# Independent products put ahead of transposes that wait, in a two-layer decoder trunk on one core

## The chip, the cores and the metric

The kernel runs on one core of a Trainium2 chip. The metric is device time in microseconds (us) of one launch, as the median of several runs; the trace comes from one profiled execution. The engines are called TensorE (PE in the profile; PEld is its weight load), VectorE (DVE), ScalarE (ACT), GpSimd (POOL) and SyncE (SP, here only a queue that issues loads).

## The reference

The input is 512 tokens of width 1024, and a memory of 256 rows. There are two layers, and everything is float32:

```python
for layer in range(2):
    x = layer_norm(a * x + 0.5 * swiglu(x, ffn_w_gu[layer, 0], ffn_w_down[layer, 0]))
    if layer == 0:   # latent attention: 12 heads from a low-rank q (256) and kv (128)
        o_tok, q_mem = mla_mix(x, ...)
    else:            # sparse attention: compressed, selected and window branches
        o_tok, q_mem = nsa_mix(x, ..., *shared)
    o_mem = memory_attention(q_mem, mem, w_mem_kv[layer])
    x = layer_norm(a * x + concat(o_tok, o_mem) @ w_out[layer])
    x = layer_norm(a * x + 0.5 * swiglu(x, ffn_w_gu[layer, 1], ffn_w_down[layer, 1]))
    if layer == 0:
        shared = nsa_shared_kv(x, nsa_w_kv, cmp_pos, cmp_w1, cmp_b1, cmp_w2)
```

In `mla_mix` one product `x @ w_in` gives the low-rank q and kv, a rotary key of 32 and the memory queries (256). The q and kv parts are normed (rms). In `nsa_shared_kv` one product gives keys and values; for the compressed branch, overlapping windows of 32 rows (stride 16) of the keys (j = 0) and of the values (j = 1) go through a small network:

```python
def compress(z, j):                       # 31 windows, two groups
    flat = (z[:, :, idx] + cmp_pos[j]).reshape(B, G, n_cmp, 32 * 64)
    return jax.nn.gelu(flat @ cmp_w1[j] + cmp_b1[j]) @ cmp_w2[j]
```

In `nsa_mix`, one product gives queries, 36 gates for each token and the memory queries.

## The kernel before, in words

A float32 product is made of three products: each operand is cast to a high half on ScalarE, VectorE subtracts it from the source to get the low half (`split`, lines 198 and 199), and TensorE adds high times high, high times low and low times high (`mm3`, lines 350 to 352, with the token tile standing still; `feature_major`, lines 362 to 367, with the weights standing still). The feed-forwards use a scheme with fewer products for part of their tiles (lines 375 to 379).

Weights arrive in units of 128 by 1024 numbers, in the fixed order of `_unit_order`. `unit(name, idx, look)` hands out the next unit and prepares up to `look` more: `prep` issues the load on SP's queue (line 129) into one of 4 raw buffers and splits it into one of 7 pairs of buffers. So a unit's load waits until a raw buffer is split, its split waits until a pair is free, and a pair is free when TensorE has made its last product with it.

The program is written in the order of the stages; a scheduler then sets the final order of each engine's instructions once, from the written order as priority and a model of its own. Each engine runs its list in order. PSUM banks are named by number, `bank(i)`. The stages are: feed-forward, memory keys, `mla_in`, latent heads, output product, feed-forward, `shared_kv`, feed-forward, `nsa_in`, sparse heads, output product, feed-forward. The change touches four places:

- **The latent step (`mla_in`).** For each of 4 token tiles t: 24 products into `bank(t)` with 416 columns; ScalarE sums squares; GpSimd takes the power; VectorE writes the scaled tile `c` (lines 762 to 771); TensorE transposes it in four pieces into `bank(4 + t)` (line 776); then `split`. Behind the loop come the two halves of the memory queries, 48 products each.
- **The compressed keys (`shared_kv`).** Behind the key products: 24 products of values for each of 4 token tiles (from the units `wvv`), then for j = 0 and 1: 48 products of the windows `zz[j]` with four units `w1`, the gelu on VectorE and ScalarE (lines 984 to 991, its result is `hb`), two transposes of `hb` (line 994), a split into `hT`, and 6 small products with the unit `w2`. Between the loads on SP's queue stand two copies of the keys (`ke`, `ko`, lines 963 and 964), each waiting for its cast.
- **Layer 1's first step (`nsa_in`).** For each token tile, 24 products of 292 columns; ScalarE takes the gates' exponential and copies the memory queries into `c` (line 1071), a buffer that it shares with the layer norms' gain and bias; TensorE transposes `c` (line 1074). Query products stand between the second and the third tile.
- **The start.** 12 products of zeros warm TensorE (line 1256), `prep()` loads the first weights, then eight pieces of the transposed input are loaded (line 1262) and split into `xhi` and `xlo`. The constants `cst` are loaded on GpSimd's queue, and VectorE casts them to `cbf` (line 1269).

Of the kernel before, what the change touches and what calls it, by code (L numbers as in the profile page):

```python
# [17 lines left out]
P = 128  # L18
T = 512
D = 1024  # L20
NT = 4
# [31 lines left out]
def _unit_order():  # L53

    order = []

    def ffn(l, f, s):
        for m0, items in _groups(l, f):
            m = m0
            for it in items:  # L60
                if it == "d":
                    order.extend((f"g{i}", (l, f, m), 1024, s) for i in range(4))
                else:
                    order.extend(("gu", (l, f, m, g), 1024, s) for g in range(2))
                m += 1
            for i in range(m0, m):
                order.append(("dn", (l, f, i), 1024, s))

    ffn(0, 0, 0)
    for l in range(2):  # L70
        for i in range(4):
            order.append(("wm", (l, i), 1024, 0))
    for i in range(4):
        order.append(("wc", (i,), 832, 0))
    for i in range(2):
        order.append(("wqm", (i,), 1024, 0))
    order.append(("wuv", (), 768, None))
    order.append(("wuk", (), 768, None))
    for i in range(3):
        order.append(("wuq", (i,), 1024, None))  # L80
    for k in MIXORDER:
        order.append(("wo", (0, k), 1024, 1))
    ffn(0, 1, 1)
    for i in range(4):
        order.append(("wkf", (i,), 1024, 1))
    for i in range(2):
        order.append(("wvv", (i,), 1024, 1))
    for j in range(2):
        for i in range(4):
            order.append(("w1", (j, i), 1024, 1))  # L90
        order.append(("w2", (j,), 256, 1))
    ffn(1, 0, 1)
    for i in range(3):
        order.append(("wgq", (i,), 876, 1))
    for i in range(6):
        order.append(("wq", (i,), 1024, 1))
    for k in MIXORDER:
        order.append(("wo", (1, k), 1024, 2))
    ffn(1, 1, 2)
    return order  # L100
# [3 lines left out]
def tile_trunk(ctx: ExitStack, tc, a: dict, out):  # L104
# [633 lines left out]
    def mla_in(cT):  # L738
        tst, tp = right_pool("mtmp", 2)
        rope = tp.tile([P, 2, NT, 32], F32, name="rope", bufs=1)  # L740
        nc.gpsimd.dma_start(rope, a["rope"])
        gbc = tp.tile([P, 384], F32, name="gbc", bufs=1)
        nc.gpsimd.dma_start(gbc[:, 0:256], a["mla_q_norm_g"].to_broadcast([P, 256]))
        nc.gpsimd.dma_start(gbc[:, 256:384], a["mla_kv_norm_g"].to_broadcast([P, 128]))
        ws = [unit("wc", (i,), 3 - i) for i in range(4)]
        for t in range(NT):
            ps = bank(t)
            q = slice(t * P, (t + 1) * P)
            for k in range(NKT):
                hi, lo = ws[k // 2]  # L750
                c = slice(k % 2 * 416, k % 2 * 416 + 416)
                mm3(ps[:, 0:416], F.xhi[:, k, q], F.xlo[:, k, q], hi[:, c], lo[:, c], k == 0, k == NKT - 1)
            ss = tp.tile([P, 2], F32, name="ss")
            junk = tp.tile([P, 256], F32, name="junk", bufs=1)
            nc.scalar.activation(junk, ps[:, 0:256], AF.Square, accum_out=ss[:, 0:1])
            nc.scalar.activation(junk[:, 0:128], ps[:, 256:384], AF.Square, accum_out=ss[:, 1:2])
            nc.vector.tensor_scalar(ss[:, 0:1], ss[:, 0:1], 1.0 / 256, RMS_EPS, op0=ALU.mult, op1=ALU.add)
            nc.vector.tensor_scalar(ss[:, 1:2], ss[:, 1:2], 1.0 / 128, RMS_EPS, op0=ALU.mult, op1=ALU.add)
            rr = tp.tile([P, 2], F32, name="rr")
            nc.gpsimd.tensor_tensor(rr, ss, mhalf, op=ALU.pow)  # L760
            c = tp.tile([P, 512], F32, name="c")
            nc.vector.scalar_tensor_tensor(c[:, 0:256], ps[:, 0:256], rr[:, 0:1], gbc[:, 0:256],
                                           op0=ALU.mult, op1=ALU.mult)
            nc.vector.scalar_tensor_tensor(c[:, 256:384], ps[:, 256:384], rr[:, 1:2], gbc[:, 256:384],
                                           op0=ALU.mult, op1=ALU.mult)
            r1 = tp.tile([P, 32], F32, name="r1")
            r2 = tp.tile([P, 32], F32, name="r2")
            nc.vector.tensor_tensor(r1, ps[:, 384:416], rope[:, 0, t, :], op=ALU.mult)
            nc.vector.tensor_tensor(r2[:, 0:16], ps[:, 400:416], rope[:, 1, t, 0:16], op=ALU.mult)
            nc.vector.tensor_tensor(r2[:, 16:32], ps[:, 384:400], rope[:, 1, t, 16:32], op=ALU.mult)  # L770
            nc.vector.tensor_tensor(c[:, 384:512].rearrange("p (n r) -> p n r", r=32),
                                    r1[:, None, :].to_broadcast([P, 4, 32]),
                                    r2[:, None, :].to_broadcast([P, 4, 32]), op=ALU.add)
            pt = bank(4 + t)
            for b in range(4):
                nc.tensor.transpose(pt[:, b * P:(b + 1) * P], c[:, b * P:(b + 1) * P], ident)
            split(cT[:, 0, :, q], cT[:, 1, :, q], pt.rearrange("p (b q) -> p b q", q=P))
        for i in range(2):
            w = unit("wqm", (i,), 2)
            ps = bank(i)  # L780
            feature_major(w, ps, 0, T)
            split(F.qm[i][:, 0, :], F.qm[i][:, 1, :], ps, scale=0.125)
        tst.close()

    def mla_heads(cT):
# [136 lines left out]
    def shared_kv(zp):  # L922
# [40 lines left out]
        nc.sync.dma_start(S.ke[64:128, 0].bitcast(F32), S.ke[0:64, 0].bitcast(F32))  # L963
        nc.sync.dma_start(S.ko[0:64, 0].bitcast(F32), S.ko[64:128, 0].bitcast(F32))
        wv = [unit("wvv", (i,), 4) for i in range(2)]
        for t in range(NT):
            p = bank(4 + t)
            q = slice(t * P, (t + 1) * P)
            for k in range(NKT):
# [1 line left out]
                c = slice(k % 4 * 256, k % 4 * 256 + 256)  # L971
                mm3(p[:, 0:256], F.xhi[:, k, q], F.xlo[:, k, q], hi[:, c], lo[:, c], k == 0, k == NKT - 1)
            nc.scalar.copy(S.v[:, t], p[:, 0:256].rearrange("p (r d) -> p r d", r=2))
        for j in range(2):
            p = bank(j)
            for i in range(4):
                hi, lo = unit("w1", (j, i), 4)
                for c in range(4):
                    k = i * 4 + c
                    mm3(p[0:64, 0:256], zz[j][:, 0, k, :], zz[j][:, 1, k, :],  # L980
                        hi[:, c * 256:c * 256 + 256], lo[:, c * 256:c * 256 + 256], k == 0, k == 15)
            hb = zp.tile([64, 256], F32, tag="hb", name="hb")
            u = zp.tile([64, 256], F32, tag="u", name="u")
            nc.vector.tensor_tensor(hb, p[0:64, 0:256], b1[:, j, :], op=ALU.add)
            nc.vector.tensor_tensor(u, hb, hb, op=ALU.mult)
            nc.vector.tensor_scalar(u, u, 0.044715, 1.0, op0=ALU.mult, op1=ALU.add)
# [2 lines left out]
            nc.vector.tensor_scalar(u, u, 1.0, None, op0=ALU.add)  # L989
            nc.vector.reciprocal(u, u)  # L990
            nc.vector.tensor_tensor(hb, hb, u, op=ALU.mult)
            pt = bank(2 + j)
            for k in range(2):
                nc.tensor.transpose(pt[:, k * 64:k * 64 + 64], hb[:, k * P:(k + 1) * P], ident[0:64, 0:64])
# [4 lines left out]
            for k in range(2):  # L999
# [2 lines left out]
                    mm3(p[:, 0:64], hi[:, w], lo[:, w], hT[:, 0, k, :], hT[:, 1, k, :], k == 0, k == 1)  # L1002
                else:
                    mm3(p[0:64, 0:128], hT[:, 0, k, :], hT[:, 1, k, :], hi[:, w], lo[:, w], k == 0, k == 1)
            if j == 0:
                for v in range(2):
                    for e in range(2):
                        r, c, n = slice(64 * e, 64 * e + 64), slice(64 * v + 32 * e, 64 * v + 32 * e + 32), 32 * e
                        split(S.kc[r, v, 0, c], S.kc[r, v, 1, c], p[r, n:n + 32])
            else:  # L1010
                for v in range(2):
                    for e in range(2):
                        r, c = 64 * v + 32 * e, slice(64 * e, 64 * e + 64)
                        nc.scalar.copy(S.vc[r:r + 32, v, c], p[32 * e:32 * e + 32, c])


    def query(pr, qf, qx):
# [39 lines left out]
    def nsa_in(gt, qf):  # L1057
# [4 lines left out]
        def gates_qmem(t):  # L1062
# [6 lines left out]
            nc.scalar.activation(gt[:, t, :], ps[:, 0:36], AF.Exp, scale=-1.0)  # L1069
            c = F.xp.tile([P, 256], F32, tag=("g", "b")[t % 2], name="c")  # L1070
            nc.scalar.copy(c, ps[:, 36:292])
            pt = bank(4 + t)
            for b in range(2):
                nc.tensor.transpose(pt[:, b * P:(b + 1) * P], c[:, b * P:(b + 1) * P], ident)
# [3 lines left out]
        def q_out(i, p):  # L1078
            split(qf[:, i, 0, :], qf[:, i, 1, :], p, scale=0.125)

        gates_qmem(0)
        gates_qmem(1)
        pq = [bank(i) for i in (0, 1, 4)]
        for i in range(3):
            feature_major(wq[i], pq[i], 0, 256)
        gates_qmem(2)
        gates_qmem(3)
        nc.vector.tensor_scalar(gt, gt, 1.0, None, op0=ALU.add)
        scores = memory_scores(lambda n: bank(5 + n % 3))
        for i in range(3):  # L1090
            feature_major(wq[i], pq[i], 256, 512)
            q_out(i, pq[i])
            next(scores)
            next(scores)
# [159 lines left out]
    pc = bank(7)  # L1254
    for i in range(12):
        nc.tensor.matmul(pc, lhsT=cold[:, 0:P], rhs=cold, start=i == 0, stop=i == 11)
    prep()
    for c in range(2):
        for e in range(2):
            xr, q = F.raw[e, c], slice(c * 256, (c + 1) * 256)  # L1260
            for i in (slice(0, 2), slice(2, 4)):
                nc.sync.dma_start(xr[:, i], a["xT"][c, e][:, i])
                k = slice(e * 4 + i.start, e * 4 + i.stop)
                split(F.xhi[:, k, q], F.xlo[:, k, q], xr[:, i])
        if c == 0:
# [206 lines left out]
```

## Time and profile before

| | before |
|---|---|
| median of 3 runs | 1878.33 us (1875.61 to 1878.87) |
| profiled execution | 1874.17 us, span 1872.2 us |
| mean granted TensorE clock | 0.997 |
| TensorE busy | 1844.3 us, 99% of the span |
| VectorE, ScalarE busy | 1466.2 us (78%), 869.8 us (46%) |

In the profile's rows a line number is that of the kernel, and often of a helper (`split` is L198 on ScalarE and L199 on VectorE). A row of a timeline has the start, the length, the engine, the line, what is written and read, and in brackets the idle time before it with what ended it. A row of the waits has the line that waited, what it waited for, the sum in us, the number of waits and the longest. In a table of stretches each engine has its busy us and its number of instructions, and behind them stand the granted clock, the share of the transfer engines and GB/s. Products overlap in the pipeline, so the rate of a group is read from start to start.

### The profile page before, as it was taken

What the parts mean: (1) busy time and instruction counts of PE and PEld (TensorE: products, weight loads), DVE (VectorE), ACT (ScalarE), POOL (GpSimd) and SP (SyncE); (2) the same over time, 40 slices, a digit from 0 to 9 for tenths busy, and PEclk for the clock granted to TensorE, in tenths of its full rate; (3) what the DMA queues carried; (4) which work ended last, traced back from release to release, by engine and by line L of the source; (5) the groups of instructions that cost most, each with busy time, mean ns of one, the idle gap of its engine ahead of it and who ended that gap; (6) DMA issues with size and microseconds to landing.
All of it is one profiled execution on the core that took longest, in us unless ns stands there. A gap on an engine that the chain in (4) does not pass through costs nothing.

```text
span 1872.2 us, 31918 instructions
## 1 busy us (share of the span) xinstructions
PE 1844.3 (99%) x12776; PEld 1650.9 (88%) x12776; DVE 1466.2 (78%) x2362; ACT 869.8 (46%) x1435; POOL 164.2 (9%) x185
## 2 busy tenths in 40 slices
PE   9999999999999999999999999999999999999998
PEld 8899899986679899899999998998956689999997
DVE  8788789757658789788797987987577478888887
ACT  5344345456545345334653433444466345434432
POOL 0000000125500000000100000001255200000000
PEclk9999999999999999999999999999999999999999
DMA  6333335521134234234433323334321224323322
GB/s 245 112 109 126 101 113 158 174 89 35 57 113 136 79 102 136 80 103 145 129 117 113 124 81 112 113 123 154 107 46 28 88 83 146 102 91 113 113 81 78
DMA packets 59700, 203.85 MB, mean 109 GB/s; under 512 B 6944, under 2 KB 7216, under 8 KB 59552
## 3 DMA queue, kind: packets, MB, share of 16 engines
q1 hardware_dynamic: 57136, 194.70, 31.7%
q0 software_dynamic: 2416, 7.11, 1.2%
q8 instruction: 101, 1.65, 0.4%
q14 instruction: 47, 0.39, 0.1%
HBM read 188.16 MB, written 7.34 MB: 104 GB/s over the span
## 4 chain that ended last, share of the span: by engine, by line
PE 92%; DVE 3%; ACT 2%; POOL 1%; issue 1%; DMA 0%; SPq 0%; POOLq 0%; DVEq 0%; ACTq 0%
PE bank L375 13%; PE bank L379 13%; PE bank L376 13%; PE bank L411 5%; PE bank L414 5%; PE bank L412 5%; PE bank L410 5%; PE bank L413 4%; PE bank L415 4%; PE bank L367 3%; PE bank L364 3%; PE bank L362 3%; PE o L645 3%; PE tb L617 3%; PE s L1153 1%; PE bank L352 1%
## 5 line engine op out<-in xcount | busy, mean ns | idle before, releaser
L198 ACT CAST whi<-wraw 128x1024 fp32r<-128x1024 f32 (+3 forms) x479 | 463.2, 976 | 539.2 <-PE bank L415 244.3
L199 DVE TENSOR_TENSOR wlo<-wraw,whi 128x1024 fp32r<-128x1024 f32 (+3 forms) x479 | 536.3, 1126 | 126.6 <-ACT whi L198 125.1
L375 PE MATMUL bank<-t,whi 128*128 128x256 f32 x1232 | 298.4, 278 | 0.0
L376 PE MATMUL bank<-t,whi 128*128 128x256 f32 x1232 | 297.9, 278 | 0.0
L376 PEld LDWEIGHTS bank<-t,whi 128*128 128x128 f32 x1232 | 231.8, 188 | 0.0
L375 PEld LDWEIGHTS bank<-t,whi 128*128 128x128 f32 x1232 | 231.8, 188 | 0.0
L376 PE MATMUL bank<-xlo,whi 128*128 128x256 f32 x924 | 221.9, 277 | 0.0
L375 PE MATMUL bank<-xhi,whi 128*128 128x256 f32 x924 | 221.8, 277 | 0.0
L379 PE MATMUL bank<-t,wlo 128*128 128x256 f32 x1232 | 191.8, 278 | 0.0
L375 PEld LDWEIGHTS bank<-xhi,whi 128*128 128x128 f32 x924 | 173.6, 188 | 0.6
L376 PEld LDWEIGHTS bank<-xlo,whi 128*128 128x128 f32 x924 | 173.6, 188 | 0.6
L379 PEld LDWEIGHTS bank<-t,wlo 128*128 128x128 f32 x1232 | 164.2, 189 | 0.0
L314 DVE SCALAR_TENSOR_TENSOR x<-x,bank 128x512 f32<-128x512 f32 x176 | 112.6, 683 | 57.1 <-PE bank L414 54.3
L379 PE MATMUL bank<-xhi,wlo 128*128 128x256 f32 x924 | 142.9, 277 | 0.0
L411 PE MATMUL bank<-whi,hhi 128*128 128x512 f32 x336 | 131.0, 390 | 0.0
L413 PE MATMUL bank<-wlo,hhi 128*128 128x512 f32 x336 | 130.9, 390 | 0.0
L410 PE MATMUL bank<-whi,hhi 128*128 128x512 f32 x336 | 130.8, 390 | 0.0
L414 PE MATMUL bank<-whi,hlo 128*128 128x512 f32 x336 | 130.8, 389 | 0.0
L412 PE MATMUL bank<-wlo,hhi 128*128 128x512 f32 x336 | 130.8, 389 | 0.0
L362 PE MATMUL bank<-xhi,whi 128*128 128x256 f32 x544 | 130.1, 280 | 0.7 <-ACT xhi L198 0.7
L364 PE MATMUL bank<-xlo,whi 128*128 128x256 f32 x544 | 130.2, 280 | 0.5 <-DVE xlo L199 0.5
L415 PE MATMUL bank<-whi,hlo 128*128 128x512 f32 x336 | 130.7, 389 | 0.0
(330 smaller groups left out, 3548.8 us busy)
## 6 DMA issues: line engine op xcount, KB each, us to landing
wraw<-in_gu SPq DMA_DIRECT2D x175, 512.0 KB, 3.3
wraw<-in_dn SPq DMA_DIRECT2D x88, 512.0 KB, 3.7
wraw<-in_wo SPq DMA_DIRECT2D x16, 512.0 KB, 3.3
wraw<-in_wm SPq DMA_DIRECT2D x8, 512.0 KB, 4.1
x_dram<-x SPq DMA_DIRECT2D x8, 512.0 KB, 3.0
x<-x_dram SPq DMA_DIRECT2D x8, 512.0 KB, 4.4
wraw<-in_w SPq DMA_DIRECT2D x8, 512.0 KB, 4.1
wraw<-in_wq SPq DMA_DIRECT2D x6, 512.0 KB, 3.3
```

Of the source, the lines that this page charges most:

```text
L198: nc.scalar.copy(hi, src)
L199: eng.tensor_tensor(lo, src, hi.bitcast(F32), op=ALU.subtract)
L364: nc.tensor.matmul(ps[:, c0:c1], lhsT=hi[:, k * P:(k + 1) * P], rhs=F.xlo[:, k, c0:c1], start=False, stop=False)
L375: nc.tensor.matmul(ps, lhsT=hi[:, ks], rhs=xh[:, k], start=k == 0, stop=False)
L376: nc.tensor.matmul(ps, lhsT=hi[:, ks], rhs=xl[:, k], start=False, stop=False)
L379: nc.tensor.matmul(ps, lhsT=lo[:, ks], rhs=xh[:, k], start=False, stop=k == 3)
L410: nc.tensor.matmul(p0, lhsT=ahi, rhs=hi[:, 0:512], start=first, stop=False)
L411: nc.tensor.matmul(p1, lhsT=ahi, rhs=hi[:, 512:1024], start=first, stop=False)
L412: nc.tensor.matmul(p0, lhsT=ahi, rhs=lo[:, 0:512], start=False, stop=False)
L413: nc.tensor.matmul(p1, lhsT=ahi, rhs=lo[:, 512:1024], start=False, stop=False)
L414: nc.tensor.matmul(p0, lhsT=alo, rhs=hi[:, 0:512], start=False, stop=last)
L415: nc.tensor.matmul(p1, lhsT=alo, rhs=hi[:, 512:1024], start=False, stop=last)
```

## The change

In the latent step and in the compressed keys the loops are split into functions, and these are called in another order; the window units' look-ahead falls from 4 to 2 and the two `w2` units move behind all `w1` units. In layer 1's first step the transposes become a function of their own, called later. At the start the loads of the first two input pieces are issued by ScalarE, ahead of the first `prep()`.

```diff
@@ _unit_order
     for j in range(2):
         for i in range(4):
             order.append(("w1", (j, i), 1024, 1))
+    for j in range(2):
         order.append(("w2", (j,), 256, 1))
@@ mla_in
-        for t in range(NT):
+        def latent(t):
...
+            return c
+
+        def turned(t, c):
+            q = slice(t * P, (t + 1) * P)
             pt = bank(4 + t)
             for b in range(4):
                 nc.tensor.transpose(pt[:, b * P:(b + 1) * P], c[:, b * P:(b + 1) * P], ident)
             split(cT[:, 0, :, q], cT[:, 1, :, q], pt.rearrange("p (b q) -> p b q", q=P))
-        for i in range(2):
+
+        def memory_query(i):
...
+        cs = [latent(0)]
+        for t in range(1, NT):
+            cs.append(latent(t))
+            turned(t - 1, cs[t - 1])
+        memory_query(0)
+        turned(NT - 1, cs[NT - 1])
+        memory_query(1)
@@ shared_kv
-        for t in range(NT):
+        def values(t):
...
-        for j in range(2):
+        def windows(j):
             p = bank(j)
             for i in range(4):
-                hi, lo = unit("w1", (j, i), 4)
+                hi, lo = unit("w1", (j, i), 2)
...
-            hb = zp.tile([64, 256], F32, tag="hb", name="hb")
-            u = zp.tile([64, 256], F32, tag="u", name="u")
+            return p
+
+        def gelu(j, p):
+            hb = zp.tile([64, 256], F32, tag=f"hb{j}", name="hb")
+            u = zp.tile([64, 256], F32, tag=f"u{j}", name="u")
...
+            return hb
+
+        def compressed(j, hb):
             pt = bank(2 + j)
...
+        values(0)
+        values(1)
+        hb = [gelu(j, windows(j)) for j in range(2)]
+        values(2)
+        compressed(0, hb[0])
+        values(3)
+        compressed(1, hb[1])
@@ nsa_in
-        gates_qmem(0)
-        gates_qmem(1)
+        c = [gates_qmem(0), gates_qmem(1)]
+        qmem(0, c[0])
         pq = [bank(i) for i in (0, 1, 4)]
-        for i in range(3):
+        feature_major(wq[0], pq[0], 0, 256)
+        qmem(1, c[1])
+        for i in (1, 2):
             feature_major(wq[i], pq[i], 0, 256)
-        gates_qmem(2)
-        gates_qmem(3)
+        c = [gates_qmem(2), gates_qmem(3)]
+        qmem(2, c[0])
+        late = [c[1]]
...
             feature_major(wq[i], pq[i], 256, 512)
+            if late:
+                qmem(3, late.pop())
@@ start
+    for i in (slice(0, 2), slice(2, 4)):
+        nc.scalar.dma_start(F.raw[0, 0][:, i], a["xT"][0, 0][:, i])
     prep()
...
-                nc.sync.dma_start(xr[:, i], a["xT"][c, e][:, i])
+                if c or e:
+                    nc.sync.dma_start(xr[:, i], a["xT"][c, e][:, i])
```

The scheduler had already moved instructions against the written order, so what the change moves is read from the built order. TensorE in the latent step before, with buffer numbers (`bank_4232` holds the second tile's products, `c_4216` is the first tile's):

```order
L350 MATMUL bank_4232<-whi_4005,xhi_3637 128x416
L776 MATMUL bank_4225<-cst_73,c_4216 128x128 x3
L351 MATMUL bank_4232<-wlo_4006,xhi_3637 128x416
L352 MATMUL bank_4232<-whi_4005,xlo_3638 128x416
L350 MATMUL bank_4232<-whi_4124,xhi_3637 128x416
L351 MATMUL bank_4232<-wlo_4125,xhi_3637 128x416
L776 MATMUL bank_4225<-cst_73,c_4216 128x128
```

and now (`bank_4225` holds the second tile's products and `bank_4274` the third's, `c_4209` is the first tile's; lines are those of the changed kernel):

```order
L352 MATMUL bank_4225<-wlo_4131,xhi_3637 128x416
L353 MATMUL bank_4225<-whi_4130,xlo_3638 128x416
L782 MATMUL bank_4267<-cst_73,c_4209 128x128 x4
L351 MATMUL bank_4274<-whi_3973,xhi_3637 128x416
L352 MATMUL bank_4274<-wlo_3974,xhi_3637 128x416
```

Before, three of a tile's transposes stand behind 10 of the next tile's 24 products and the fourth 4 products later; now all four stand behind all 24. The last tile's transposes move from the middle of the first memory query behind its 48 products.

TensorE around the first transposes of the compressed keys, before:

```order
L351 MATMUL bank<-wlo,zh 64x256
L352 MATMUL bank<-whi,zh 64x256
L994 MATMUL bank<-cst,hb 128x64 x2
L350 MATMUL bank<-hT,whi 128x64
L351 MATMUL bank<-hT,whi 128x64
L352 MATMUL bank<-hT,wlo 128x64
```

and now:

```order
L353 MATMUL bank<-whi,xlo 128x256
L351 MATMUL bank<-whi,xhi 128x256
L1017 MATMUL bank<-cst,hb 128x64 x2
L352 MATMUL bank<-wlo,xhi 128x256
L353 MATMUL bank<-whi,xlo 128x256
L351 MATMUL bank<-whi,xhi 128x256
L352 MATMUL bank<-wlo,xhi 128x256
L351 MATMUL bank<-hT,whi 128x64
```

Before, the transposes stand right behind the 96 window products. Now the 24 value products of the third tile and 7 of the fourth stand between; 4 more products stand between the transposes and the first product with `hT`, and 10 more ahead of the other five. The second window's transposes stand behind 31 products of the next feed-forward now, where there were 77.

VectorE in the same place, before:

```order
L984 TENSOR_TENSOR hb<-bank,b_9741 64x256
L985 TENSOR_TENSOR u<-hb 64x256
L986 TENSOR_SCALAR u<-u 64x256
L199 TENSOR_TENSOR wlo<-wraw,whi 128x1024
L987 TENSOR_TENSOR u<-u,hb 64x256
L389 TENSOR_TENSOR wraw<-b 128x1024
L989 TENSOR_SCALAR u<-u 64x256
L990 RECIPROCAL u<-u 64x256
L199 TENSOR_TENSOR wlo<-wraw,whi 128x1024
L991 TENSOR_TENSOR hb<-hb,u 64x256
```

and now (`L390` and `L389` of before make a combination of input blocks for the feed-forward):

```order
L1006 TENSOR_SCALAR u<-u 64x256
L1007 TENSOR_TENSOR u<-u,hb 64x256
L200 TENSOR_TENSOR wlo<-wraw,whi 128x1024
L390 TENSOR_TENSOR wraw<-b 128x1024
L1009 TENSOR_SCALAR u<-u 64x256
L1004 TENSOR_TENSOR hb<-bank,b_9741 64x256
L1010 RECIPROCAL u<-u 64x256
L1005 TENSOR_TENSOR u<-hb 64x256
L1011 TENSOR_TENSOR hb<-hb,u 64x256
```

The second window's first steps (L1004, L1005) now stand among the first window's last ones, and a unit's low half moves out from between the reciprocal and the last step. Ahead of the first L1004 all eight `w1` units are split. On SP's queue seven `w1` loads stand ahead of the copies of the keys, and one `w1` and both `w2` loads behind them, where six `w1` and one `w2` stood ahead and two `w1` and one `w2` behind. In layer 1's first step the first transposes stay where they were, behind the second tile's products.

More of the change, by code (lines that the diff above doesn't have):

```diff
@@ L1004, in shared_kv @@
                     mm3(p[0:64, 0:128], hT[:, 0, k, :], hT[:, 1, k, :], hi[:, w], lo[:, w], k == 0, k == 1)
-            if j == 0:
-                for v in range(2):
-                    for e in range(2):
+            for v in range(2):
+                for e in range(2):
+                    if j == 0:
                         r, c, n = slice(64 * e, 64 * e + 64), slice(64 * v + 32 * e, 64 * v + 32 * e + 32), 32 * e
                         split(S.kc[r, v, 0, c], S.kc[r, v, 1, c], p[r, n:n + 32])
-            else:
-                for v in range(2):
-                    for e in range(2):
+                    else:
                         r, c = 64 * v + 32 * e, slice(64 * e, 64 * e + 64)
                         nc.scalar.copy(S.vc[r:r + 32, v, c], p[32 * e:32 * e + 32, c])
+        values(0)
[5 more added lines that the diff above has]
+        compressed(1, hb[1])
     def query(pr, qf, qx):
@@ L1071, in gates_qmem, with qmem @@
             nc.scalar.copy(c, ps[:, 36:292])
+            return c
+        def qmem(t, c):
+            q = slice(t * P, (t + 1) * P)
             pt = bank(4 + t)
```

## The prediction

> **What bounds the kernel now.** I read the page first: shares of the span, then the chain that ended last.
>
> ```profile
> PE 1844.3 (99%) x12776; PEld 1650.9 (88%) x12776; DVE 1466.2 (78%) x2362; ACT 869.8 (46%) x1435; POOL 164.2 (9%) x185
> PE 92%; DVE 3%; ACT 2%; POOL 1%; issue 1%; DMA 0%; SPq 0%; POOLq 0%; DVEq 0%; ACTq 0%
> wraw<-in_gu SPq DMA_DIRECT2D x175, 512.0 KB, 3.3
> wraw<-in_w SPq DMA_DIRECT2D x8, 512.0 KB, 4.1
> ```
>
> TensorE is the bound nearly everywhere, and the change takes no product away. It can only win what TensorE waits, and what the clock loses after a wait. The last two lines (issue to landing of a load, in us) are used further down. Next I read what TensorE waits for, summed by line:
>
> ```profile
> PE bank L776 <- DVE c L762: 2.8, 4, 0.7
> PE bank L994 <- DVE hb L991: 2.4, 1, 2.4
> PE bank L362 <- ACT xhi L198: 0.7, 1, 0.7
> PE bank L364 <- DVE xlo L199: 0.5, 1, 0.5
> PE bank L1074 <- ACT c L1071: 0.5, 1, 0.5
> ```
>
> L776 is the transposes of the latent step (layer 0's attention), L994 those of the compressed keys, L1074 those of layer 1's attention, L362/L364 here the kernel's very first products. Together the four places hold 2.8 + 2.4 + 0.5 + 1.2 = 6.9 us, so this list alone caps the change; the timelines add what it doesn't hold.
>
> **Part 1, the latent step.** TensorE's timeline around the first tile's transposes (start, length, work, wait):
>
> ```profile
> 377.59 0.34 PE L350 MATMUL bank<-whi,xhi 128*128 128x416 f32 x1
> 378.56 0.59 PE L776 MATMUL bank<-cst,c 128*128 128x128 f32 x3 [0.63 <-DVE c L762]
> 378.90 0.44 PE L351 MATMUL bank<-wlo,xhi 128*128 128x416 f32 x1
> 379.18 0.35 PE L352 MATMUL bank<-whi,xlo 128*128 128x416 f32 x1
> 379.37 0.35 PE L350 MATMUL bank<-whi,xhi 128*128 128x416 f32 x1
> ```
>
> and VectorE's last write of that tile:
>
> ```profile
> 379.06 0.29 DVE L771 TENSOR_TENSOR c<-r,r 128x128 f32<-128x128 f32 x1
> ```
>
> The order of before puts three transposes behind 10 of the next tile's 24 products. Products start 0.19 apart (379.18 to 379.37). Around the transposes it is 378.90 - 377.59 = 1.31; 0.19 for the product and 0.34 for the transposes (378.56 to 378.90) leave 0.78 lost, where the wait is given as 0.63. So the four tiles lose 2.8 by the list of waits, or 2.8 x 0.78/0.63 = 3.5 from start to start; I take 3.1. In the new order all 24 products stand ahead. The next tile began at 377.59 - 9 x 0.19 = 375.9, so its transposes would come at 375.9 + 24 x 0.19 = 380.4, while c is written by 379.06 + 0.29 = 379.35: 1.05 us of slack. The last tile stands behind the 48 products of the first memory query instead, at some 0.12 each (as the values' below) 5.8 us. No DMA or queue is moved. What is late next is VectorE's split of the transposes, which the heads need only after the second memory query. **Gain 3.1 (2.8 to 3.5).**
>
> **Part 2, the compressed keys.** TensorE before, from the first value product to the next feed-forward:
>
> ```profile
> 924.68 0.28 PE L350 MATMUL bank<-whi,xhi 128*128 128x256 f32 x1
> ...
> 935.99 0.28 PE L350 MATMUL bank<-whi,zh 128*64 128x256 f32 x1
> ...
> 946.77 0.28 PE L352 MATMUL bank<-whi,zh 128*64 128x256 f32 x1
> 949.46 0.31 PE L994 MATMUL bank<-cst,hb 64*128 64x64 f32 x2 [2.42 <-DVE hb L991]
> 950.12 0.30 PE L350 MATMUL bank<-hT,whi 128*128 128x64 f32 x1 [0.35 <-ACT hT L198]
> 950.70 0.30 PE L351 MATMUL bank<-hT,whi 128*128 128x64 f32 x1 [0.28 <-DVE hT L199]
> ...
> 951.28 0.36 PE L362 MATMUL bank<-xhi,whi 128*128 128x256 f32 x1
> ```
>
> Idle: 2.42 + 0.35 + 0.28 = 3.05 us. The 96 value products take (935.99 - 924.68)/96 = 0.118 each, the 96 window products (946.77 - 935.99)/95 = 0.113. The clock drops just behind it; stretches of the trace, with TensorE's busy time and its granted clock (PEclk):
>
> ```profile
> 947.00:951.30 4.30, 1.25 (x10) 0.98 (x9) 4.30 (x7) 2.76 (x4) 0.00 (x0) 1.00 0.31 87
> 951.30:962.00 10.70, 10.70 (x81) 10.57 (x80) 9.86 (x17) 3.24 (x7) 0.00 (x0) 0.84 0.21 65
> 952.00:956.00 4.00, 4.00 (x24) 4.00 (x23) 3.87 (x10) 1.66 (x5) 0.00 (x0) 0.57 0.41 131
> 962.00:972.00 10.00, 10.00 (x89) 9.85 (x89) 9.16 (x11) 7.51 (x13) 0.00 (x0) 1.00 0.26 88
> ```
>
> TensorE was busy 1.25 of 4.30 us; then 81 products in 10.70 us, where the next stretch's rate (89 in 10) makes 95. The 14 missing ones cost 14 x 10/89 = 1.6 us. The whole fall lies in 952.0 to 956.0 (4.0 x 0.43 = 1.7 as 10.7 x 0.16 = 1.7), right behind the waits, and is in no list of them.
>
> Now the new order: values 0 and 1, windows 0, windows 1, values 2, 7 products of values 3, then the transposes. From 924.68: 48 x 0.118 = 930.3; 96 x 0.113 = 941.2; (24 + 7) x 0.118 = 944.9, where hb has to be there. VectorE's and the loads' rows of before, for its chain:
>
> ```profile
> 931.48 0.54 SPq L129 DMA_DIRECT2D wraw<-in_w  x1
> ...
> 934.78 1.05 ACT L198 CAST whi<-wraw 128x1024 fp32r<-128x1024 f32 x1 [1.04 <-PE bank L352]
> ...
> 941.64 0.42 DVE L984 TENSOR_TENSOR hb<-bank,b 64x256 f32<-64x256 f32 x1
> ...
> 944.71 1.21 DVE L389 TENSOR_TENSOR wraw<-b 128x1024 f32<-128x1024 f32 x1
> ...
> 946.16 1.75 DVE L990 RECIPROCAL u<-u 64x256 f32<-64x256 f32 x1
> 947.83 1.15 DVE L199 TENSOR_TENSOR wlo<-wraw,whi 128x1024 fp32r<-128x1024 f32 x1
> ```
>
> The order puts the last w1 unit's low half ahead of hb's first step, and its load behind the two copies of the keys on SP's queue, whose releases the change leaves alone: issue 931.5, + 4.1 landing = 935.6, cast 1.05 = 936.7, low half 1.2 = 937.9. TensorE needs that unit at 930.3 + 84 x 0.113 = 939.8, so it hides. Then four gelu steps and two quarter-size splits, 0.4 each as L984 or less: 940.2. The first gate unit's low half is next: its raw buffer comes free when the third unit of the second window is split, about 935.7; + 3.3 landing + 1.05 cast = 940.1, + 1.15 = 941.2. L389 1.2, one short step 0.3, the other window's first step 0.4 (its products end at 941.2), reciprocal 1.75, two steps of 0.4: 945.65. TensorE comes at 944.9, so a new wait of 0.7 us takes the place of 2.4. If the gate unit lands 1 us later (4.3, like the in_w loads) it is 1.6; if these steps overlap more tightly, 0.4. The waits for hT go behind 4 and 14 products (0.47 and 1.65 us). The second window's hb now meets 31 products of the feed-forward: by the same chain it is about 0.3 late (0 to 0.5). Idle saved: 3.05 - 0.7 - 0.3 = 2.05. With two short waits among products instead of 3 us in 4.3, I take the clock's 1.6 as saved too. **Gain 3.7 (1.0 to 4.3).**
>
> A rule of the Trainium skill stands against that last term. "TensorE: Matmul & The Clock Gate", section "HAM oscillation — how this bites in real kernels", wants idle gaps of more than about 3.4 us before the clock falls. The longest gap here is 2.42, and the clock fell all the same; by the rule the fall has another cause and stays, and the part would be worth 2.05. I go by the row, as the fall stands within 1.3 us of the last wait's end (950.70).
>
> **Part 3, layer 1's first step.** The 0.5 us wait of the first transposes (L1074 above) stays: the order of those instructions is as before, and their input is written into a buffer that the layer norm of the last tile still reads. The later transposes move past 19 to 24 products, but the list of waits shows them no wait. **0 (-0.3 to +0.3).**
>
> **Part 4, the start.** The queues, ScalarE, VectorE and TensorE there:
>
> ```profile
> 0.73 0.87 SPq L129 DMA_DIRECT2D wraw<-in_gu  x2
> 1.65 1.85 SPq L1262 DMA_DIRECT2D b<-in_xT  x4
> 3.75 1.30 ACT L198 CAST whi<-wraw 128x512 fp32r<-128x512 f32 x2 [1.74 <-DMA wraw<-in_gu]
> 5.86 0.29 DVE L1269 CAST cbf<-cst 128x256 bf16<-128x256 f32 x1 [4.73 <-DMA cst<-in_cst]
> 6.07 1.29 DVE L199 TENSOR_TENSOR wlo<-wraw,whi 128x512 fp32r<-128x512 f32 x2
> 7.27 2.73 DVE L199 TENSOR_TENSOR xlo<-b,xhi 128x512 fp32r<-128x512 f32 x4
> ...
> 8.02 0.38 PE L364 MATMUL bank<-xlo,whi 128*128 128x256 f32 x1 [0.48 <-DVE xlo L199]
> ```
>
> The two loads leave SP's queue and start 0.9 us earlier (0.73 for 1.65), which makes xhi early; their issue on ScalarE's queue, about 2 x 0.46, pushes its table load back, and the 1.74 us that it waits for the first weight hide that. But L364 needs xlo, and VectorE reaches xlo only after the cast of the constants, which waits for their own load on POOL's queue until 5.86. From there it runs without a gap. The order on VectorE is unchanged, so nothing is won: **0**, with -0.9 if the constants land later by as much as these loads go earlier, and +1.2 if they land early and both waits (0.7 and 0.5) go.
>
> **The sum.** 3.1 + 3.7 + 0 + 0 = 6.8 us. The profiled execution took 1874.17 (span 1872.2), so its like would take 1867.4; the median of the runs is 1878.33 (1875.61 to 1878.87), 4.2 above that execution, and from it 1871.5.
>
> **The rivals.**
> - *The half-clock window stays*, by the rule above or because windows fall otherwise: for it, that the trace has another such window, in layer 1's attention, that this change doesn't touch (a clock of 0.54):
>
> ```profile
> 1375.30:1379.00 3.70, 3.70 (x12) 1.75 (x11) 0.42 (x1) 3.67 (x14) 0.55 (x1) 0.54 0.47 113
> ```
>
> Against it, the fall's place right behind the waits. Gain 5.2, 1873.1. Chance 0.22.
> - *VectorE becomes the bound in the compressed keys*: hb 1.6 late, the second 0.5, and so the half clock stays. For it: VectorE is busy all 4.30 us of 947.0 to 951.3, and the same work must now be done earlier. Gain 3.1 + 3.05 - 2.1 = 4.05, 1874.3, on the edge of what can be told; with the start's -0.9, 1875.2. Chance 0.20.
> - *Slower: the last w1 unit comes late.* It is needed 5.6 us earlier than before by TensorE and still stands behind the keys' copies on SP. Slack is 939.8 - 937.9 = 1.9. A delay d costs d - 1.9, and the half clock stays (gain of the rest 5.2). It decides from d = 7.1; at d = 11 the time is 1878.33 - 5.2 + 9.1 = 1882.2. Against it: nothing on the way of the keys' copies is moved. Chance 0.05.
> - *The change doesn't do what it says* holds for parts 3 and 4 and is in the sum already.
>
> **Chances and range.** The forecast has 0.53. About 0.2%, 3.8 us, is what a measurement of this kernel tells from no change. Faster by more: the forecast, nine tenths of the first rival, a fifth of the second: 0.77. Slower 0.05, the rest 0.18. Low end: part 1 3.5, part 2 4.3, the rest 1.5, the other half-clock window gone by luck 1.6 = 10.9, or 1867.4; half a microsecond for the spread of runs: 1867. High end: the second rival with the start's loss, 1875.2, and 0.8 for the spread: 1876.
>
> **What would show it.** Right: no wait of the latent transposes for c; at the compressed keys a wait for hb under 1 us; no clock under 1.00 in the 12 us behind it; the feed-forward's first product 5 us earlier than before. The 0.5 us wait at layer 1's gates and L364 at about 8.0 unchanged. Wrong: a wait for w1's halves inside the second window, hb over 1.5 late, a new stretch of half clock anywhere, or the constants landing after 6.5 us.

## The result, and the profile after

| | before | after |
|---|---|---|
| median, first comparison (4 runs each) | 1878.6 us (1875.61 to 1881.42) | 1868.99 us (1868.63 to 1869.39) |
| ratio, with 95% interval | | 0.9949 (0.9932 to 0.9966) |
| median, second comparison (13 and 5 runs) | 1876.67 us (1873.92 to 1879.93) | 1869.33 us (1867.69 to 1874.03) |
| ratio, with 95% interval | | 0.9964 (0.9952 to 0.9977) |
| profiled execution, span | 1874.17 us, 1872.2 us | 1869.39 us, 1867.5 us |

The kernel is faster, by 9.6 us in the first comparison (6.4 to 12.8 by the interval) and by 6.8 in the second (0.0036 x 1876.67; 4.3 to 9.0). The forecast was 6.8. The profiled executions differ by only 4.8 us: the execution of before that was profiled lies below all four of its timed runs, and a part below shows why.

The page after, the same two lines as before:

```profile
PE 1842.7 (99%) x12776; PEld 1651.6 (88%) x12776; DVE 1465.6 (78%) x2362; ACT 869.4 (47%) x1435; POOL 164.3 (9%) x185
PE 89%; DVE 4%; ACT 2%; issue 2%; POOL 1%; DMA 1%; POOLq 0%; DVEq 0%; ACTq 0%
```

TensorE is as busy as it was, as no product was taken away. What it waits for after, at the places of the change (the line, what it waited for, us in all, times, longest):

```profile
PE bank L363 <- ACT xhi L199: 1.3, 1, 1.3
...
PE bank L365 <- DVE xlo L200: 1.2, 1, 1.2
...
PE bank L1017 <- DVE hb L1011: 0.7, 1, 0.7
...
PE bank L1107 <- ACT c L1100: 0.5, 1, 0.5
```

The latent step's transposes (L782 now) are gone from the list. The compressed keys' wait fell from 2.4 to 0.7, layer 1's stayed at 0.5, and the two waits at the start grew from 0.7 and 0.5 to 1.3 and 1.2.

The latent step on TensorE, and VectorE's last write of the first tile, after:

```profile
381.51 0.35 PE L353 MATMUL bank<-whi,xlo 128*128 128x416 f32 x1
381.69 0.60 PE L782 MATMUL bank<-cst,c 128*128 128x128 f32 x4
382.05 0.43 PE L351 MATMUL bank<-whi,xhi 128*128 128x416 f32 x1
```

```profile
380.34 0.29 DVE L773 TENSOR_TENSOR c<-r,r 128x128 f32<-128x128 f32 x1
```

The tile is whole at 380.63, TensorE comes to it at 381.69: 1.06 us of slack, where the forecast had 1.05. There is no bracket, so no wait.

The compressed keys on TensorE, and VectorE's steps that set `hb`, after:

```profile
944.08 0.30 PE L1017 MATMUL bank<-cst,hb 64*128 64x64 f32 x2 [0.74 <-DVE hb L1011]
945.27 0.30 PE L351 MATMUL bank<-hT,whi 128*128 128x64 f32 x1 [0.24 <-ACT hT L199]
946.67 0.19 PE L352 MATMUL bank<-hT,whi 128*128 128x64 f32 x1
```

```profile
934.89 1.23 DVE L200 TENSOR_TENSOR wlo<-wraw,whi 128x1024 fp32r<-128x1024 f32 x1 [0.80 <-ACT whi L199]
936.15 0.42 DVE L1004 TENSOR_TENSOR hb<-bank,b 64x256 f32<-64x256 f32 x1
...
938.65 1.23 DVE L200 TENSOR_TENSOR wlo<-wraw,whi 128x1024 fp32r<-128x1024 f32 x1 [0.21 <-ACT whi L199]
...
941.59 1.73 DVE L1010 RECIPROCAL u<-u 64x256 f32<-64x256 f32 x1
...
943.53 0.40 DVE L1011 TENSOR_TENSOR hb<-hb,u 64x256 f32<-64x256 f32 x1
```

The chain runs as it was laid out: the last window unit's low half, four gelu steps, the gate unit's low half (it waited 0.21 for its cast), the reciprocal, the last step. The new wait is 0.74, where 0.7 was forecast. The stretches behind it:

```profile
941.00:945.00 4.00, 3.26 (x27) 2.87 (x25) 4.00 (x8) 2.72 (x5) 0.00 (x0) 1.00 0.37 151
945.00:957.00 12.00, 11.76 (x103) 11.53 (x103) 11.32 (x20) 7.58 (x19) 0.00 (x0) 1.00 0.28 89
```

TensorE was busy 3.26 of 4.00 us, and the clock is 1.00 throughout; the stretch at half clock is gone in this execution.

### The profile page after: what moved, and what is told of

The parts are those of the page before. It is cut to its first block, busy times and chain, and to the rows that moved or that the text cites. A ratio compares the mean times of both kernels' runs of the same rounds, so it can differ in the third digit from the quotient of the medians.

```text
span 1867.5 us, 31922 instructions
## 1 busy us (share of the span) xinstructions
PE 1842.7 (99%) x12776; PEld 1651.6 (88%) x12776; DVE 1465.6 (78%) x2362; ACT 869.4 (47%) x1435; POOL 164.3 (9%) x185
## 4 chain that ended last, share of the span: by engine, by line
PE 89%; DVE 4%; ACT 2%; issue 2%; POOL 1%; DMA 1%; POOLq 0%; DVEq 0%; ACTq 0%
PE bank L376 13%; PE bank L380 13%; PE bank L377 13%; PE bank L415 4%; PE bank L411 4%; PE bank L413 4%; PE bank L412 4%; PE bank L414 4%; PE bank L416 4%; PE o L646 3%; PE bank L365 3%; PE bank L368 3%; PE bank L363 3%; PE tb L618 3%; PE s L1191 1%
```

## The experiments

Eleven runs were made in three groups, each group on one chip beside the kernel before. The stages were also measured in the traces, from the start of one product to the start of another: the latent step from its first product of 416 columns to the heads' first product, and the keys from the last transpose of the layer norm ahead of them to the next feed-forward's first product with a combination of input blocks.

| run | 24th product of the kernel at | latent step | keys | wait for hb | half clock behind it |
|---|---|---|---|---|---|
| before | 11.3 | 35.3 | 66.6 | 2.4 | 3.4 us |
| e1, latent step alone | 12.6 | 31.7 | 67.2 | 2.4 | 6.8 us |
| e3, start alone | 13.0 | 35.3 | 65.8 | 2.5 | 3.4 us |
| e4, layer 1 alone | 12.7 | 35.3 | 67.8 | 2.6 | 6.8 us |
| e5, wait filled | 13.7 | 35.3 | 66.2 | none | none |
| e2, keys alone | 13.5 | 35.6 | 64.4 | 2.0 | 3.4 us |
| after | 12.6 | 31.7 | 62.7 | 0.7 | none |
| e9, after again | 11.2 | 31.7 | 62.3 | 0.8 | none |
| e7, after without start | 12.8 | 31.7 | 63.2 | 0.9 | none |
| e6, after, 20 zeros | 11.3 | 31.7 | 64.5 | 2.1 | 3.4 us |
| e11, the same again | 11.4 | 31.7 | 62.2 | 1.3 | none |
| e8, e7 with 20 zeros | 11.8 | 31.7 | 63.3 | 1.1 | none |
| e10, values ahead | 12.3 | 31.7 | 62.9 | none | none |

### One part at a time

The first group takes each part of the diff alone on top of the kernel before. Its kernel before had 1877.62 us (31 runs, 1873.15 to 1880.56).

**e1**, the latent step:

```diff
+        cs = [latent(0)]
+        for t in range(1, NT):
+            cs.append(latent(t))
+            turned(t - 1, cs[t - 1])
+        memory_query(0)
+        turned(NT - 1, cs[NT - 1])
+        memory_query(1)
```

> Only the latent step's new order. Theory A (waits alone, additive): 3.6 us off between the step's start and the heads, as in the trace of the whole change, and 3 to 4 us off the median, 1874.5 to 1875.5 against 1878.5. Theory B (the part also removes a fall of the clock that before has in most of its runs, though not in the profiled one): 5 us or more off the median, and a spread of its runs under 2 us where before has 6.

Measured: 1873.14 us (9 runs, 1871.72 to 1875.06), ratio 0.9973 (0.9963 to 0.9982), so 3.4 to 6.9 us off. The stage is 3.6 us shorter in the trace, in every trace with the new order (31.7 against 35.3). The median is between the two theories and its interval holds the 3.6, so what lies beyond that is not shown. It is no proof of theory B: the mean granted clock of its runs is that of before (median 0.996 of 9 runs and of 31), the spread of its runs is 3.3 us, not under 2, and the fall of the clock behind the keys was still there, and twice as long as in the trace of before:

```profile
943.50:947.20 3.70, 0.92 (x6) 0.47 (x4) 3.70 (x5) 2.97 (x4) 0.00 (x0) 1.00 0.08 18
947.20:954.10 6.90, 6.61 (x32) 6.60 (x32) 6.63 (x16) 2.19 (x6) 0.00 (x0) 0.51 0.43 148
```

That is the row by which the profiled execution of before was a kind one: the same wait cost it 3.4 us at half clock, and in e1 and e4 6.8.

**e2**, the compressed keys:

```diff
+        values(0)
+        values(1)
+        hb = [gelu(j, windows(j)) for j in range(2)]
+        values(2)
+        compressed(0, hb[0])
+        values(3)
+        compressed(1, hb[1])
```

> Only the compressed keys' new order. Theory A (the idle 3.05 us become 0.7 to 1.2, and the half-clock window behind them goes): 3.9 us off, with no clock under 1.00 behind the keys. Theory C (the half-clock window has another cause and stays): 2.3 us off, with a window at half clock within 12 us of the transposes.

Measured: 1873.2 us (11 runs, 1869.79 to 1876.76), ratio 0.9977 (0.9968 to 0.9986), 2.6 to 6.0 us off. Its profiled execution is its slowest, 1876.76, and has the late `hb` of the prediction's second rival. Waits of TensorE, then the gate unit's load on SP's queue and its cast:

```profile
PE bank L1003 <- DVE hb L997: 2.0, 1, 2.0
```

```profile
940.96 1.02 SPq L130 DMA_DIRECT2D wraw<-in_gu  x1
```

```profile
945.14 1.05 ACT L199 CAST whi<-wraw 128x1024 fp32r<-128x1024 f32 x1 [1.20 <-DMA wraw<-in_gu]
```

From issue to cast the load took 4.2 us, where in the trace after it took 3.45 (934.12 to 937.57). That is one half of the longer wait. Counted from the last transpose of the layer norm ahead, as in the table, `hb` was whole at 34.2 us (33.5 in the trace after), and TensorE came to its transposes at 32.3 (32.9 in the trace after), as its key products and first values started 0.113 apart in this execution and 0.118 in that one. The half clock followed:

```profile
949.90:953.30 3.40, 1.65 (x14) 1.61 (x15) 3.40 (x7) 1.97 (x5) 0.00 (x0) 1.00 0.00 1
953.30:956.80 3.50, 3.50 (x19) 3.50 (x18) 3.50 (x5) 2.09 (x5) 0.00 (x0) 0.51 0.68 207
```

Theory A's 3.9 lies in the interval. Its clause on the clock holds only where the wait stays short: of the seven traces with this order (e10 left out, its order differs) five have a wait of 0.7 to 1.3 and full clock, two a wait of 2.0 or 2.1 and 3.4 us at half clock. The second of the two is e6, and there it was another load: the gate unit's cast came as early as in the trace after, but the last `w1` unit took 5.2 us from issue to cast (927.61 to 932.82), where the other six took 3.8 to 4.0, and VectorE began `hb` 1.2 us later:

```profile
932.82 1.05 ACT L199 CAST whi<-wraw 128x1024 fp32r<-128x1024 f32 x1 [2.95 <-DMA wraw<-in_w]
```

The stage is 62.7 us on average in the five and 64.4 in the two, 1.7 apart. Half of 3.4 us is as much, but the two also waited 1.1 longer and ran their first products at the shorter pitch, so the 1.7 is not the clock's alone.

**e3**, the two loads:

```diff
+    for i in (slice(0, 2), slice(2, 4)):
+        nc.scalar.dma_start(F.raw[0, 0][:, i], a["xT"][0, 0][:, i])
     prep()
```

> Only the two loads on ScalarE's queue. Theory A (constants land 0.5 us later because the first loads share the transfer engines with them, so xlo is 0.5 us later): the 24th product at 11.0 us instead of 9.9, 0.5 to 1.3 us slower than before. Rival: the later start in the trace of the whole change is chance of that execution (when the clock's window falls), and alone the part gives 0 +- 0.3 in the position of the first xlo product (8.0).

Measured: 1876.76 us (11 runs), ratio 0.9992 (0.9983 to 1.0001). Theory A's slower time is not borne out, nor is a gain shown. Its start was late all the same: the first product with xlo came at 8.9 (the rival had 8.0 +- 0.3) and the 24th at 13.0 (11.3 in the trace of before by the same count), with half clock from 8.6 to 12.0. Its VectorE at the start:

```profile
6.74 0.29 DVE L1272 CAST cbf<-cst 128x256 bf16<-128x256 f32 x1 [5.61 <-DMA cst<-in_cst]
6.95 1.29 DVE L199 TENSOR_TENSOR wlo<-wraw,whi 128x512 fp32r<-128x512 f32 x2
8.15 1.29 DVE L199 TENSOR_TENSOR xlo<-b,xhi 128x512 fp32r<-128x512 f32 x2
```

The constants' cast starts at 6.1 to 6.7 in the six traces with the two loads moved (6.74 here, 6.33 on average) and at 5.5 to 6.5 in the seven with the loads as they were (6.02 on average). The way that theory A named, xlo behind the constants, is seen; the size of the harm, if there is one, is lost in the spread from execution to execution.

**e4**, layer 1's first step: `qmem(0)` and `qmem(1)` around the first query products, `qmem(2)` and `qmem(3)` behind the gates.

> Only layer 1's first step's new order. Theory A: the wait of 0.5 us for the memory queries' copy stays, nothing else moves: 0 +- 0.5 us. Rival: the moved transposes change what follows (pitch of the products from start to start, 0.113 or 0.118 us), 0.5 to 1 us either way from 1300 us on.

Measured: 1878.11 us (11 runs), ratio 0.9997 (0.9988 to 1.0006). The wait is where it was:

```profile
PE bank L1078 <- ACT c L1071: 0.5, 1, 0.5
```

Theory A holds within some 2 us, and nothing here is shown to be won. The rival's 0.5 to 1 us either way is below what these runs can tell.

The parts' medians lie 4.5, 4.4 and 0.9 below and 0.5 above that of before, 9.3 in sum. By the traces it is 3.6 for the latent step, 3.6 for the keys (66.8 on average in before, e1, e3 and e4; 63.2 in the seven) and nothing that shows elsewhere, 7.2. Both sums lie in the interval of the first comparison of the whole change, and 7.2, not 9.3, in that of the second.

### Is the fall of the clock due to the wait?

**e5** leaves the order of before and fills the wait with products that nothing reads:

```diff
+            if j == 1:
+                fill = bank(6)
+                for n in range(20):
+                    nc.tensor.matmul(fill[:, 0:256], lhsT=F.xhi[:, n % 8, 0:128],
+                                     rhs=F.xhi[:, n % 8, 0:256], start=n == 0, stop=n == 19)
```

> The order of before, with 20 products of 256 columns whose result is not read put into the wait of the compressed keys' transposes (20 x 0.118 = 2.4 us, the length of the wait). They save no wait; they only keep TensorE busy. Theory A (the clock falls behind the wait because TensorE idles): no clock under 1.00 within 12 us of the transposes, and 1.6 to 3 us off the median, 1875 to 1876 where before has 1877.6. Theory C (the fall has another cause, or a gap under 3.4 us cannot be it): a window at half clock stays and the median is that of before within 0.7 us.

Measured: 1873.63 us (11 runs) beside 1876.2 (18 runs), ratio 0.9986 (0.9977 to 0.9995), so 0.9 to 4.3 us off by products that do nothing but keep TensorE busy. The stretches that answer to those of before:

```profile
947.00:951.30 4.30, 4.30 (x40) 4.30 (x38) 4.27 (x6) 3.60 (x6) 0.00 (x0) 1.00 0.42 170
951.30:962.00 10.70, 9.96 (x82) 9.52 (x82) 10.54 (x20) 4.38 (x9) 0.00 (x0) 1.00 0.29 100
```

TensorE is busy through the wait, and the clock is 1.00 where it was 0.84. So theory A holds and theory C falls: the idle time was the cause. The mean granted clock of all runs says the same: 0.996 to 0.999 (median 0.998) in the 11 runs with the fill, 0.995 to 0.997 (median 0.996) in the 18 of before beside them. The stage itself is only 0.6 us shorter than the 66.8 of the four. In this execution the 225 products from the feed-forward's first one to the end of the stage start 0.118 us apart, where three of the four have 0.113 to 0.114 (median steps), and that takes back some 225 x 0.005 = 1.1 us.

The traces also show where 3.4 us at half clock in one execution and 6.8 in another come from. In each trace the clock changes only at steps of a grid of 3.413 us, and this grid lies differently against the kernel's start in each execution. In the trace of before the wait falls across two windows of the grid:

```profile
945.29:948.71 3.42, 1.75 (x16) 1.50 (x14) 3.38 (x4) 2.88 (x3) 0.00 (x0) 1.00 0.33 135
948.71:952.12 3.41, 2.02 (x15) 1.80 (x16) 3.41 (x7) 1.50 (x4) 0.00 (x0) 1.00 0.58 162
```

and in e1 almost whole into one:

```profile
943.83:947.24 3.41, 0.61 (x4) 0.39 (x3) 3.41 (x5) 2.64 (x4) 0.00 (x0) 1.00 0.09 18
```

TensorE is busy 0.51 and 0.59 of the two windows, and one window at half clock follows; it is busy 0.18 of the one, and two follow. e3 (0.46 and 0.62) is like before, and e4 (0.14) is like e1; in e2 (0.49) and e6 (0.56) one follows. The half-clock window in layer 1's attention, which the prediction's first rival had for it, stands behind idle time too, in the trace of before:

```profile
1371.96:1375.37 3.41, 1.36 (x10) 0.87 (x9) 2.34 (x4) 0.53 (x3) 2.30 (x3) 1.00 0.01 2
```

It is there in ten of the thirteen traces, each time behind a window with TensorE busy 0.40 to 0.50; in e2, e5 and e6 the idle time there falls across two windows, busy 0.67 to 0.72 each, and the clock stays full. So that row spoke for idle time as the cause, and not against it. Where between these shares the clock falls is not settled: in e10 a window with 0.53 busy was followed by full clock.

### The start

In the profiled execution of before the clock stayed full from 8 us on; in eight of the ten traces with 12 products of zeros there is a half-clock window of 3.4 us or more between 7.8 and 15 us. After, two stretches of the start:

```profile
4.80:8.20 3.40, 1.28 (x5) 0.38 (x3) 1.84 (x4) 2.62 (x6) 0.00 (x0) 1.00 1.04 409
8.20:11.60 3.40, 3.08 (x14) 3.09 (x15) 3.40 (x6) 2.56 (x4) 0.00 (x0) 0.50 1.03 413
```

The zeros end, TensorE waits for xhi and xlo (1.28 busy of 3.40), and the clock falls to 0.50. **e6** and **e11** are the whole change with more zeros, and **e7** and **e8** a pair without the two loads:

```diff
-    for i in range(12):
-        nc.tensor.matmul(pc, lhsT=cold[:, 0:P], rhs=cold, start=i == 0, stop=i == 11)
+    for i in range(20):
+        nc.tensor.matmul(pc, lhsT=cold[:, 0:P], rhs=cold, start=i == 0, stop=i == 19)
```

> The whole change, with 20 instead of 12 products of zeros at the start, which then last to about 8 us, when the first low half of the input is there. Theory A (the half-clock window that four of five traces show at 8 to 12 us follows the idle 2.4 us between the zeros and the second product): clock 1.00 from there on, the 24th product at 11.0 instead of 12.6, 1.5 us off: 1867.5. Rival: the zeros run past the arrival of the input and cost what they win: 1869 +- 0.5.

> The whole change without the two loads on ScalarE's queue. If these loads delay the constants (first xlo 7.98 on average in two traces against 7.60 in four): 0.4 us faster than the whole change, 1868.6. If their median alone (0.9 us under before) is their effect: 1869.9. Neither is told apart for sure; 1869 +- 1.

> As before this one, with 20 products of zeros at the start. Theory A: first products at full clock, 1.5 us under the same kernel with 12: 1867.1 to 1868.4. Rival: no difference.

> The whole change with 20 products of zeros at the start, beside the whole change on the same chip. Theory A: the clock is full from 8 us on and 1.5 to 2 us go, as in the pair without the two loads (1871.2 and 1869.1). Rival: no difference, as the first timing of the whole change (1869.0) against this one (1868.8) looks, though on different chips or days.

The stretches of e11:

```profile
4.80:8.20 3.40, 3.40 (x11) 1.25 (x10) 1.89 (x4) 2.73 (x6) 0.00 (x0) 1.00 1.04 408
8.20:11.60 3.40, 3.40 (x27) 3.19 (x26) 3.40 (x6) 2.57 (x4) 0.00 (x0) 1.00 1.03 414
```

In all three traces with 20 zeros the clock is full from 8 us on, and the 24th product starts at 11.3 to 11.8 where the other ten have 11.2 to 13.7. The runs:

| | median | ratio to before |
|---|---|---|
| e7, without the two loads, 12 zeros | 1871.17 (7 runs) | 0.997 (0.9959 to 0.998) |
| e8, the same, 20 zeros | 1869.09 (5 runs) | 0.9959 (0.9947 to 0.9972) |
| e6, whole change, 20 zeros | 1868.79 (6 runs) | 0.9962 (0.995 to 0.9974) |
| e9, whole change | 1869.33 (5 runs) | 0.9964 (0.9952 to 0.9977) |
| e11, whole change, 20 zeros | 1868.19 (6 runs) | 0.996 (0.9947 to 0.9973) |

The mechanism is shown by the clock. The gain is 2.1 us between e7 and e8 and 1.1 between e9 and e11, in the expected direction and near the expected 1.5 to 2, but the intervals overlap, so it is not clear of noise. Taken alone, the medians missed their forecasts: e6 lies in its rival's range (1868.5 to 1869.5) and not at theory A's 1867.5, and e7 and e8 lie 1.2 and 0.7 us above theirs. e11 has the lowest median measured. What the two loads are worth is not resolved: e6 and e8 are 0.3 apart, and e3's interval reaches from 0.2 us slower to 3.2 faster.

### The whole change again, and one more product group ahead

> The whole change again, with more runs than the first time, beside the next two. If the parts add (4.5 + 4.4 + 0.9 - 0.5 of the medians): 9 us off, ratio 0.995. If they add as the traces have them (3.7 in the latent step, 4 to 5 at the keys, nothing at the start): 7.5 to 8.5 off, ratio 0.9955 to 0.996. A wait of 0.7 to 1.2 for hb in its trace.

Measured: 0.9964 (0.9952 to 0.9977), which is nearer to the sum by the traces. **e10** puts the fourth tile's values ahead of the first transposes too:

```diff
         values(2)
-        compressed(0, hb[0])
         values(3)
+        compressed(0, hb[0])
         compressed(1, hb[1])
```

> The whole change, but the values of the fourth tile stand ahead of the first window's transposes too. Theory A (VectorE's chain sets both hb): the first wait (0.7) goes, the waits for hT (0.6) come back since nothing stands between, and the second window's transposes come 3 us earlier, after 14 products of the feed-forward, and wait 1.8 us for their hb: 1.4 us slower than the whole change, with a half-clock window possible behind it. Rival (more products ahead of the transposes are always better): 0.7 us faster.

Measured: 1872.19 us (7 runs), ratio 0.9976 (0.9966 to 0.9987), against 0.9964 for e9: 2.2 us slower by the ratios, with overlapping intervals; its profiled execution, 1869.3, is its fastest. The first wait did go, and the wait came back one step later, though not where theory A put it. TensorE, then ScalarE:

```profile
PE bank L351 <- ACT hT L199: 1.6, 1, 1.6
...
PE bank L352 <- DVE hT L200: 0.4, 1, 0.4
```

```profile
945.61 0.42 ACT L1008 ACTIVATE u<-u 64x256 f32<-64x256 f32 x1 [1.82 <-DVE u L1007]
945.94 0.35 ACT L989 COPY sv<-bank 128x256 f32<-128x256 f32 x1
946.19 0.26 ACT L199 CAST hT<-bank 128x128 fp32r<-128x128 f32 x1
```

The cast of `hT` stands on ScalarE behind the second window's exponential, which waited 1.82 us for VectorE. The rival, more products ahead are always better, is not supported.

## Why the prediction was right

- **The time.** 1871.5 was forecast, 1867 to 1876; 1868.99 and 1869.33 were measured. The forecast's sign and place were right, and its 6.8 us lies in both intervals. That the second comparison gives 6.8 to the digit is luck, as the two comparisons differ by 2.8. Of the signs it named, those at the latent step, the keys and layer 1 came as said. Three others did not: the first product with xlo came at 8.5, not 8.0; a new stretch of half clock stands at 8.2 to 11.6; and the feed-forward's first product came 3.7 us earlier (947.58 for 951.28), not 5. The half clock at the start is also in e1 and e4, which leave the start as it was, and with it the 24th product came 1.3 us later here, which the 5 us did not reckon with.
- **Part 1, the latent step.** The mechanism and the slack (1.05 against 1.06) were right; the term was undersized. It was 3.1, with 2.8 to 3.5 as bounds, and the stage is 3.6 us shorter in every trace with the new order. The step that failed is "leave 0.78 lost": it stopped at the first product behind the transposes. From one tile's transposes to the next, before took 5.98 us (384.54 - 378.56):

```profile
384.54 0.59 PE L776 MATMUL bank<-cst,c 128*128 128x128 f32 x3 [0.75 <-DVE c L762]
```

  and after takes 4.96:

```profile
386.65 0.60 PE L782 MATMUL bank<-cst,c 128*128 128x128 f32 x4
```

  That is 1.02 for a tile. In the rows that the prediction shows, the product after the three transposes is followed only 0.28 later (378.90 to 379.18), not 0.19, and the fourth transpose breaks the stream a second time.
- **Part 2, the keys.** The forecast wait of 0.7 measured 0.74 and 0.8 in two executions of the same kernel, and the gain of 3.7 is 3.6 on average. What the bounds left out: "if the gate unit lands 1 us later it is 1.6" kept TensorE's arrival fixed, but in e2, e6 and e11 it came 0.7 us sooner, at the shorter pitch, so that e2 waited 2.0 with `hb` only 0.6 later; and the last `w1` unit, which was given 1.9 us of slack against TensorE, also holds up VectorE's chain, where 1.2 us of delay made `hb` 0.7 later (e6, a wait of 2.1). The forecast of 0.3 for the second window was not needed; its transposes show no wait.
- **The clock.** The fall behind the wait is the wait's own (e5). The Trainium skill's "TensorE: Matmul & The Clock Gate", section "HAM oscillation — how this bites in real kernels", puts the limit at idle gaps of about 3.4 us; here the clock fell in all six traces with a wait for hb of 2.0 to 2.6 us and in none with 0.7 to 1.3 (nor in e10, with 1.6 and 0.4 one after the other), so in this kernel the measurement decides against that figure. What the forecast missed is that the cost is 1.6 us or twice that, with the place of the wait on the clock's grid in that execution.
- **Part 3.** Right: the wait of 0.5 stayed (e4).
- **Part 4.** No effect clear of noise, as forecast. The constants landed 0.3 us later on average, and the bounds of -0.9 and +1.2 hold e3's median (0.9 faster) but not its whole interval. That the start has its own half-clock window in most executions was not seen, because the one trace of before was among those without.
- **The base.** The sum was made against an execution 4.2 us under the median. The traces now show where such a difference can come from: half-clock windows at the start, one or two of them behind the keys, and the pitch below.

## What to carry to other kernels

When the next products are independent, put as many of them ahead of a transpose as its input takes to arrive, and check what the chain behind it waits for next; one group too many only moved the wait to another engine's queue (e10). Read the cost of a wait from start to start over a whole period, as the products behind each break in the stream start late too. A wait of a few microseconds can cost as much again in clock, and by a different amount in each execution, so compare several traces before a term of a microsecond is believed.

## What the runs showed of the hardware

- The clock fell to half for one or two windows of 3.413 us behind single waits of 2.0 to 2.6 us, two where the wait lay almost whole in one window of the grid (e1, e4), and 20 products that nothing reads kept it at 1.00 (e5).
- The same product of 256 columns starts every 0.113 us in some stretches and every 0.118 in others, at full clock. Over one stretch of the second feed-forward before and after, with the same work:

```profile
573.00:593.00 20.00, 20.00 (x179) 20.00 (x178) 19.08 (x21) 13.37 (x16) 0.00 (x0) 1.00 0.35 114
```

```profile
573.00:593.00 20.00, 20.00 (x172) 20.00 (x171) 18.63 (x22) 12.05 (x15) 0.00 (x0) 1.00 0.42 132
```

  179 products against 172 in 20 us, TensorE never idle: about 1 us given back over the 26 us in which the trace after ran slower there. What sets the pitch was not tried and stays open.
- From issue to cast, the same load took 3.45 us in one execution and 4.2 in another (the gate unit, after and e2), and 3.8 to 5.2 (the last `w1` unit in seven traces). Together with the pitch ahead of the wait that was enough to bring the half clock back in two of seven.
